# Moving every transpose off the matrix engine: 32x32 squares on VectorE and spreading DMAs in a two-layer encoder trunk

## The chip, the cores and the metric

One core of a Trainium2 chip runs the whole kernel. The metric is device time in microseconds from the start to the end of one execution, as the median of three runs. All arithmetic is float32; matrix products are made in three passes over numbers split into a high part (rounded to the matrix engine's fp32r form) and a low part (the rest).

## The reference, cut to what matters

There are 256 tokens of width 2048, and two layers with pre-norm residuals. The two layers, cut to their core:

```
# even layer
u = rms_norm(h, ln_even_g);  qa, ka, va, qb, kb, vb, gate = split(u @ w_in_even)   # 2048 x 6656
ya = gqa_attention(rope(norm(qa)), rope(norm(ka)), va)                # 8 heads of 128, 2 kv heads
p  = softmax(q1 k1^T*s + bias) - lam * softmax(q2 k2^T*s + bias)      # 8 differential heads, 64 wide
yb = rms_norm(p @ vb, b_subln_g, eps) * (1 - lambda_init)
h  = h + (concat(ya, yb) * silu(gate)) @ w_out_even                   # 2048 x 2048
# odd layer
u = rms_norm(h, ln_odd_g);  qc, kc, vc, gate = split(u @ w_in_odd)    # 2048 x 8192
yc = attention over three dilated windows, 16 heads (a mask and one softmax in the kernel)
h  = h + (yc * silu(gate)) @ w_out_odd;   out = rms_norm(h, final_norm_g)
```

## The kernel before, in words

**Weights.** `job_t` (L163) computes 256 tokens by 512 output columns. Two PSUM banks of the pool `acc` (four banks, so two jobs at a time) take one 128-token tile each. The 2048 rows of the weight come in eight groups. `wgroup` (L135) fetches a group, 128x1024 floats or 512 KB, by one DMA on SyncE's queue into one of four `raw` slots. ScalarE copies it to `hi` (L151), VectorE subtracts to make `lo` (L152), both into one of three slots. Then `mm3` (L157) issues three matmuls of 512 columns for each of 2 k-blocks and 2 token tiles, so twelve for each group. The activations (`u` in layer inputs, `y` in output projections) are the stationary operand.

**Heads.** The projections come out token-major, tokens on partitions. Attention needs q and k with the head width on partitions, and the softmax weights with the keys on partitions. Each such turn is four TensorE transposes of 128x128 against `ident` into one PSUM bank of the pool `att`: `turned` (L228) for a pair of heads' q, k or gate (45 calls), `transposed` (L312) for the weights of one head (32 calls), L388 and L392 for the value rows and norms of the differential heads (`head_b`), and L534 for `tok` at the end of the even layer. ScalarE and VectorE then split the bank into hi and lo (`split`, L208).

`weighted_v` (L328) and `head_b` make the weighted values transposed, width on partitions and 256 tokens in the columns: six matmuls of 256 columns for each head.

**Order.** The instructions are issued in an order that a planner makes from its own costs when the program is built; each engine then keeps that order. Weight splits have raised priority. Heads are spread between the matmuls of the projection that the planner finds ready. SyncE's queue carries weight loads, inputs and the output; SyncE also stands still in order when a load waits for its slot.

In the even layer, for each of two groups: q, gate, four heads of kind A, gate, q, k, value projection, four differential heads. In the odd layer, for each of four groups: gate, q, k, softmax weights of four heads, values, weighted values. After each layer comes the output projection in chunks of columns, each of which goes through all sixteen heads.

Of the kernel before, what the change touches and what calls it, by code (L numbers as in the profile page):

```python
# [10 lines left out]
F32 = mybir.dt.float32  # L11
# [82 lines left out]
def trunk(ctx, tc, x, xt, w_even, w_oe, w_odd, w_oo, gain_cols, rows, final_g, rope_c, geo_c, out):  # L94
# [24 lines left out]
    ones = const.tile([P, P], F32, name="ones")  # L119
    G.memset(ones, 1.0)  # L120
    ident = const.tile([P, P], F32, name="ident")
    make_identity(nc, ident)
# [40 lines left out]
    def job_t(w, c0, wd, a, beside=None, pieces=lambda kg: 1):  # L163

        kn = 1024 // wd
        ps = [acc.tile([P, 512], F32, tag="acc", name=f"acc_t{t}")[:, :wd] for t in range(NT)]
        for kg in range(NK // kn):
# [25 lines left out]
    def square_sum(part, src):  # L193
        sq = work.tile([P, 512], F32, tag="sq", name="sq", bufs=1)[:, :src.shape[-1]]
        A.activation(sq, src, AF.Square, accum_out=part)
# [32 lines left out]
    def turned(z, pair):  # L228

        ps = att.tile([P, 512], F32, tag="att", name="zt")  # L230
        for j in range(2):
            for t in range(NT):
                c = (2 * pair + j) * HD
                T.transpose(ps[:, j * S + t * P:j * S + (t + 1) * P], z[:, t, c:c + HD], ident)  # L234
        return ps.rearrange("p (j k) -> p j k", j=2)

    def pair_t(z, pair, tag, bufs=2):
        ps = turned(z, pair)
        dst = heads.tile([P, 2, 2, S], F32R, tag=tag, name=tag, bufs=bufs)
        split(dst[:, :, 0], dst[:, :, 1], ps)  # L240
        return dst

    def pair_gate(z, pair):
        ps = turned(z, pair)
        gt = heads.tile([P, 2, S], F32, tag="gate", name="gate", bufs=3)
        A.copy(gt, ps)
        return gt
# [3 lines left out]
    def pair_q64(z, pair):  # L251
        ps = turned(z, pair)
        t = heads.tile([P, 2, 2, S], F32R, tag="q", name="q", bufs=2)
        for j in range(2):
            js, other = slice(64 * j, 64 * j + 64), slice(64 - 64 * j, 128 - 64 * j)
            A.activation(t[js, :, j], ps[js], AF.Copy)
            V.tensor_sub(t[other, :, j], ps[js], f(t[js, :, j]))
        return t

    def pair_k64(z, pair):  # L260
        ps = turned(z, pair)
        kh = heads.tile([P, 2, 2, S], F32R, tag="k", name="kh", bufs=2)
        kl = heads.tile([P, 2, 2, S], F32R, tag="k", name="kl", bufs=2)
        for j in range(2):
            js, other = slice(64 * j, 64 * j + 64), slice(64 - 64 * j, 128 - 64 * j)
            A.activation(kh[js, :, j], ps[js], AF.Copy)
            A.activation(kh[other, :, j], ps[js], AF.Copy)
            V.tensor_sub(kl[js, :, j], ps[js], f(kh[js, :, j]))
            A.activation(kl[other, :, j], f(kl[js, :, j]), AF.Copy)
# [19 lines left out]
    def scores(sp, qh, ql, kh, kl):  # L289
        for t in range(NT):  # L290
            ts = slice(t * P, (t + 1) * P)
            o = sp[:, t * S:(t + 1) * S]
            T.matmul(o, qh[:, ts], kh, start=t == 0, stop=False)  # L293
            T.matmul(o, qh[:, ts], kl, start=False, stop=False)  # L294
            T.matmul(o, ql[:, ts], kh, start=False, stop=t == NT - 1)  # L295
# [16 lines left out]
    def transposed(p, ps):  # L312
        for kt in range(NT):
            for t in range(NT):
                T.transpose(ps[:, kt * S + t * P:kt * S + (t + 1) * P], p[:, t, kt * P:(kt + 1) * P], ident)  # L315
        ph = heads.tile([P, NT, S], F32R, tag="ph", name="ph")
        pl = heads.tile([P, NT, S], F32R, tag="pl", name="pl")
        pv = ps.rearrange("p (t k) -> p t k", t=NT)
        split(ph, pl, pv)
        return ph, pl  # L320

    def finish_y(h, src, gate):
        yf = work.tile([P, S], F32, tag="yf", name="yf")
        V.tensor_mul(yf, src, gate)
# [3 lines left out]
    def weighted_v(h, p, v, vs, gate, ps):  # L328
        ph, pl = transposed(p, ps)
        o = ps[:, :S]  # L330
        for kt in range(NT):
            mm3(o, v[:, kt, 0, vs], v[:, kt, 1, vs], ph[:, kt], pl[:, kt], kt == 0, kt == NT - 1)
        finish_y(h, o, gate)

    def head_a(h, q, k, v, vs, gate):
        ps = bank()
        sp = scores(ps, q[:, 0], q[:, 1], k[:, 0], k[:, 1])
# [4 lines left out]
        weighted_v(h, p, v, vs, gate, ps)  # L342
# [32 lines left out]
    def head_b(h, p, v, vs, gate):  # L375
        ps = [bank(), bank()]
        ph, pl = transposed(p, ps[0])
        o = ps[1][:, :S]
        for kt in range(NT):
            mm3(o, v[:, kt, 0, vs], v[:, kt, 1, vs], ph[:, kt], pl[:, kt], kt == 0, kt == NT - 1)  # L380

        on = work.tile([P, S], F32, tag="on", name="on")
        A.copy(on, o)
        ss = small.tile([P, NT], F32, tag="ss", name="ss")
        ot, rb = ps[0][:, :S], ps[0][:, S:]
        for t in range(NT):
            ts = slice(t * P, (t + 1) * P)
            T.transpose(ot[:, ts], on[:, ts], ident)  # L388
            square_sum(ss[:, t:t + 1], ot[:, ts])
        r = rsqrt_mean(ss, HD, SUBLN_EPS, NT, "rb")  # L390
        for t in range(NT):
            T.transpose(rb[:, t * P:(t + 1) * P], r[:, t:t + 1].to_broadcast([P, P]), ident)  # L392
        V.scalar_tensor_tensor(on, on, gsub[:, 0:1], gate, op0=ALU.mult, op1=ALU.mult)
        finish_y(h, rb, on)

    def softmax_c(h, q, k):
        bias = alibi(float(np.exp2(np.float32(-8.0 * (h + 1) / 16))), True)
        sp = scores(bank(), q[:, 0], q[:, 1], k[:, 0], k[:, 1])
        p = biased(sp, bias)
# [68 lines left out]
    def tok_heads(ps, i, n):  # L468
# [3 lines left out]
        for t in range(NT):  # L472
            A.activation(z[:, t], ps[t][:, :n * HD], AF.Copy, scale=rstd[:, t:t + 1])
            sq = work.tile([P, 512], F32, tag="sq", name="sq", bufs=1)[:, :n * HD]
# [22 lines left out]
    for g in range(2):  # L497
        c = 512 * g
        zq = tok_heads(job_t(w_even, c, 512, u) if g else ps_q0, 0, 4)
        zg = gate_t(job_t(w_even, GATE_E + c, 512, u), rh)  # L500
        for pair in range(2):
            q = pair_t(zq, pair, "q")
            gate = pair_gate(zg, pair)
            for j in range(2):
                head_a(4 * g + 2 * pair + j, q[:, j], k_a[:, g], v_a[:, 0], slice(g * HD, g * HD + HD), gate[:, j])
        zg = gate_t(job_t(w_even, GATE_E + 1024 + c, 512, u), rh)
        zq = evac_t(job_t(w_even, B_Q0 + c, 512, u), rs)
        zk = evac_t(job_t(w_even, B_K0 + c, 512, u), rstd)
        v = v_tile()
        ps = []  # L510
        for pair in range(2):
            q = pair_q64(zq, pair)
            kh, kl = pair_k64(zk, pair)
            ps += [softmax_b(4 * g + 2 * pair + j, q[:, j], kh[:, j], kl[:, j]) for j in range(2)]
        evac_v(v, job_t(w_even, B_V0 + c, 512, u), rstd)
        for pair in range(2):
            gate = pair_gate(zg, pair)
            for j in range(2):
                head_b(8 + 4 * g + 2 * pair + j, ps[2 * pair + j], v[:, pair], slice(j * HD, j * HD + HD), gate[:, j])
# [6 lines left out]
    for i, (c0, wd) in enumerate(CHUNKS_E):  # L526
        ps = job_t(w_oe, c0, wd, y_even)
        cs = slice(c0, c0 + wd)
        for t in range(NT):
            V.tensor_add(tok[:, t, cs], tok[:, t, cs], ps[t])  # L530
        for k in range(c0 // P, (c0 + wd) // P):
            ps = att.tile([P, 512], F32, tag="att", name="xps")
            for t in range(NT):
                T.transpose(ps[:, t * P:(t + 1) * P], tok[:, t, k * P:(k + 1) * P], ident)  # L534
            make_u(k, ps[:, :S], gcol[:, NK + k:NK + k + 1])
# [4 lines left out]
    for g in range(4):  # L540
# [4 lines left out]
        zg = gate_t(ps, rh)  # L545
# [94 lines left out]
```

## Time and profile before

| | |
|---|---|
| median of three runs | 920.06 us (919.68 to 920.17) |
| the profiled execution's own time | 919.56 us |
| its span, first to last instruction | 917.8 us |
| TensorE matmul busy | 907.0 us, 99% of the span |
| VectorE busy | 559.6 us, 61% |
| ScalarE busy | 532.6 us, 58% |
| GpSimd busy | 78.2 us, 9% |
| busy share of the 16 DMA engines, SyncE's queue | 50.7% |

1.8 us of the execution's time lie outside the span. Busy times of matmuls overlap, since a matmul's recorded duration includes the pipeline; the distance from one start to the next says what a matmul costs in a row of them.

### The profile page before, as it was taken

The numbers are of one execution on the slowest core, as the hardware profiler recorded it, in microseconds if no ns is written. First come the engines' busy times: TensorE is split into PE (matmuls) and PEld (weight loads), VectorE is DVE, ScalarE is ACT, GpSimd is POOL, SyncE is SP. The second block draws the span as 40 slices with busy tenths as digits, with TensorE's granted clock in tenths as the row PEclk, the third lists the DMA queues.
The fourth block names the chain that finished last, engine by engine and source line by source line (L and its number), as shares of the span: only waits on it lengthen the run. The fifth ranks groups of instructions, "written<-read, shape, count | busy, mean of one in ns | idle before, by whom it ended". The sixth has DMA issues, their size and how long they took to land.

```text
span 917.8 us, 11973 instructions
## 1 busy us (share of the span) xinstructions
PE 907.0 (99%) x4440; PEld 760.4 (83%) x4440; DVE 559.6 (61%) x751; ACT 532.6 (58%) x866; POOL 78.2 (9%) x67
## 2 busy tenths in 40 slices
PE   9999999999999999999999999999999999999996
PEld 7888888888888887888888888888888888888886
DVE  6685644875766686655544765467445754476563
ACT  7657645875576696555544755456544844474451
POOL 0010000110100012000000400032001300040000
PEclk9999999999999999999999999999999999999999
DMA  8855455354544443455555445543554455555552
GB/s 329 311 211 160 154 189 184 138 189 161 179 160 160 171 151 116 169 198 183 184 201 189 154 144 192 196 162 138 186 194 170 147 174 193 193 170 179 194 196 92
DMA packets 47035, 164.39 MB, mean 179 GB/s; under 512 B 5376, under 2 KB 6144, under 8 KB 46976
## 3 DMA queue, kind: packets, MB, share of 16 engines
q1 hardware_dynamic: 46656, 162.57, 50.7%
q0 software_dynamic: 320, 1.05, 0.5%
q8 instruction: 35, 0.57, 0.3%
q14 instruction: 24, 0.20, 0.1%
HBM read 161.50 MB, written 2.10 MB: 178 GB/s over the span
## 4 chain that ended last, share of the span: by engine, by line
PE 96%; ACT 1%; issue 1%; DMA 1%; SPq 0%; DVE 0%; POOLq 0%; POOL 0%; DVEq 0%; ACTq 0%
PE acc_t L160 29%; PE acc_t L161 29%; PE acc_t L159 29%; PE zt L234 2%; PE bank L315 1%; PE bank L159 1%; PE bank L161 1%; PE bank L160 1%; DMA raw<-in_w_in_even 1%; PE bank L294 1%; PE bank L295 1%; PE bank L293 1%; ACT hi L151 0%; PE bank L363 0%; PE bank L364 0%
## 5 line engine op out<-in xcount | busy, mean ns | idle before, releaser
L152 DVE TENSOR_TENSOR lo<-raw,hi 128x1024 fp32r<-128x1024 f32 (+1 forms) x294 | 359.3, 1223 | 284.1 <-ACT hi L151 283.8
L151 ACT ACTIVATE hi<-raw 128x1024 fp32r<-128x1024 f32 (+1 forms) x294 | 309.4, 1054 | 307.7 <-PE acc_t L161 292.0
L160 PE MATMUL acc_t<-lo,u 128*128 128x512 f32 x928 | 364.9, 395 | 0.1
L161 PE MATMUL acc_t<-hi,u 128*128 128x512 f32 x928 | 362.2, 392 | 0.0
L159 PE MATMUL acc_t<-hi,u 128*128 128x512 f32 x928 | 338.4, 393 | 0.4 <-ACT u L183 0.4
L160 PEld LDWEIGHTS acc_t<-lo,u 128*128 128x128 f32 x928 | 174.6, 188 | 36.2 <-DVE lo L152 0.6
L159 PEld LDWEIGHTS acc_t<-hi,u 128*128 128x128 f32 x928 | 174.0, 188 | 36.1 <-ACT u L183 1.2
L161 PEld LDWEIGHTS acc_t<-hi,u 128*128 128x128 f32 x928 | 174.5, 188 | 33.9
L160 PE MATMUL acc_t<-lo,y 128*128 128x512 f32 (+1 forms) x256 | 96.5, 379 | 0.0
L161 PE MATMUL acc_t<-hi,y 128*128 128x512 f32 (+1 forms) x256 | 95.4, 377 | 0.0
L159 PE MATMUL acc_t<-hi,y 128*128 128x512 f32 (+1 forms) x256 | 90.4, 381 | 0.7 <-ACT hi L151 0.6
L351 POOL TENSOR_SCALAR bias<-geo 128x512 f32<-128x512 f32 x24 | 37.5, 1562 | 572.8 <-DVE s L346 534.3
L160 PEld LDWEIGHTS acc_t<-lo,y 128*128 128x128 f32 x256 | 48.3, 189 | 8.6
L159 PEld LDWEIGHTS acc_t<-hi,y 128*128 128x128 f32 x256 | 47.6, 188 | 9.4 <-ACT hi L151 1.4
L161 PEld LDWEIGHTS acc_t<-hi,y 128*128 128x128 f32 x256 | 48.2, 188 | 8.3
L304 ACT ACTIVATE s<-s,nm 128x256 f32<-128x256 f32 x64 | 31.7, 497 | 4.4 <-DVE nm L301 4.3
L216 ACT ACTIVATE z<-acc_t,rstd 128x512 f32<-128x512 f32 x40 | 27.2, 680 | 9.0 <-PE acc_t L161 9.0
L234 PE MATMUL zt<-ident,z 128*128 128x128 f32 x180 | 29.7, 272 | 0.0
L234 PEld LDWEIGHTS zt<-ident,z 128*128 128x128 f32 x180 | 22.4, 140 | 5.0
L346 DVE TENSOR_TENSOR s<-bank,bias 128x512 f32<-128x512 f32 x32 | 21.7, 682 | 6.9 <-POOL bias L353 4.4
L353 POOL TENSOR_TENSOR bias<-bias,geo 128x512 f32<-128x512 f32 x16 | 23.8, 1490 | 1.3
L210 DVE TENSOR_TENSOR pl<-bank,ph 128x512 fp32r<-128x512 f32 x32 | 21.4, 682 | 2.3 <-ACT ph L209 2.2
(137 smaller groups left out, 696.3 us busy)
## 6 DMA issues: line engine op xcount, KB each, us to landing
raw<-in_w_in_odd SPq DMA_DIRECT2D x128, 512.0 KB, 3.2
raw<-in_w_in_even SPq DMA_DIRECT2D x102, 512.0 KB, 3.3
raw<-in_w_out_even SPq DMA_DIRECT2D x32, 512.0 KB, 3.2
raw<-in_w_out_odd SPq DMA_DIRECT2D x32, 512.0 KB, 3.2
tok<-in_x SPq DMA_DIRECT2D x4, 512.0 KB, 8.8
xk<-in_xt SPq DMA_DIRECT2D x6, 256.0 KB, 6.7
raw<-in_w_in_even SPq DMA_DIRECT2D x4, 256.0 KB, 4.0
gf<-in_final_norm_g POOLq DMA_DIRECT2D x4, 256.0 KB, 4.7
```

The costliest lines, as they stand in the source:

```text
L151: A.activation(hi[:, ks], rv[:, ks], AF.Copy)
L152: splits.append(V.tensor_sub(lo[:, ks], rv[:, ks], f(hi[:, ks])))
L159: T.matmul(ps, ah, bh, start=start, stop=False)
L160: T.matmul(ps, ah, bl, start=False, stop=False)
L161: T.matmul(ps, al, bh, start=False, stop=stop)
L210: V.tensor_sub(lo, src, f(hi))
L216: A.activation(z[:, t], ps[t], AF.Copy, scale=r[:, t:t + 1])
L234: T.transpose(ps[:, j * S + t * P:j * S + (t + 1) * P], z[:, t, c:c + HD], ident)
L304: A.activation(e[:, t], s[:, t], AF.Exp, bias=nm[:, t:t + 1], accum_out=den[:, t:t + 1])
L346: V.tensor_add(s, sp, bias)
L351: G.tensor_scalar_mul(b, geo[:, 0], -slope)
L353: G.tensor_add(b, b, geo[:, 1])
```

## The change

All 372 TensorE transposes go. The new `turned` takes a 128 x 2 x 256 token-major tile. Two VectorE transposes, of 256 elements on each partition, turn every 32x32 square of it into a scratch tile `x` (two slots). Four DMAs on SyncE's queue, one for each 32 source partitions, then spread it over all 128 partitions of `pt` (three slots) or `gate`; each moves 64 KB in 128 pieces of 512 bytes. The readers that split into hi and lo now read this tile in SBUF, in an order of quarters.

The differential heads make their weighted values token-major, with the turned weights stationary and 128 value columns moving (twelve matmuls for each head), so their norm needs no turning; the finished product of a pair of heads is turned once. Queries and gates are turned sooner, while a later projection runs. The output projections start with two column chunks for the first twelve heads and then do the last four heads for both (`jobs_out`). To make room, `raw` has three slots in place of four.

```diff
-        raw = wpool.tile([P, 1024], F32, tag="raw", name="raw", bufs=4)
+        raw = wpool.tile([P, 1024], F32, tag="raw", name="raw", bufs=3)
...
+    def jobs_out(w, chunks, a):
+
+        (c0, wd), (c1, _) = chunks[:2]
+        ps = [job_banks(wd) for _ in range(2)]
+        for kgs in (range(6), range(6, 8)):
+            for p, c in zip(ps, (c0, c1)):
+                job_steps(p, w, c, wd, a, kgs)
+        for i, (c, wd) in enumerate(chunks):
+            yield i, slice(c, c + wd), ps[i] if i < 2 else job_t(w, c, wd, a)
...
-    def turned(z, pair):
-
-        ps = att.tile([P, 512], F32, tag="att", name="zt")
-        for j in range(2):
-            for t in range(NT):
-                c = (2 * pair + j) * HD
-                T.transpose(ps[:, j * S + t * P:j * S + (t + 1) * P], z[:, t, c:c + HD], ident)
-        return ps.rearrange("p (j k) -> p j k", j=2)
+    def turned(src, tag="pt", bufs=3):
+
+        x = work.tile([P, 4, 4, 32], F32, tag="x", name="x", bufs=2)
+        for m in range(2):
+            V.transpose(x[:, :, 2 * m:2 * m + 2].rearrange("p b t c -> p t b c"),
+                        src[:, :, m * P:(m + 1) * P].rearrange("p t (r b) -> p t b r", b=4))
+        dst = heads.tile([P, 4, 4, 32], F32, tag=tag, name=tag, bufs=bufs)
+        for a in range(4):
+            nc.sync.dma_start(dst[:, a].rearrange("p n c -> p (n c)"), x[32 * a:32 * a + 32].rearrange("r b n c -> r (b n c)"))
+        return dst.rearrange("p a n c -> p n a c")
...
-    def pair_gate(z, pair):
-        ps = turned(z, pair)
-        gt = heads.tile([P, 2, S], F32, tag="gate", name="gate", bufs=3)
-        A.copy(gt, ps)
-        return gt
...
+    def pair_b(h, ps, v, zg):
+
+        os = []
+        ss = small.tile([P, 8], F32, tag="ss8", name="ss4", bufs=2)[:, :2 * NT]
+        for j in range(2):
+            ph, pl = weights_t(ps[j])
+            vs = slice(j * HD, j * HD + HD)
+            o = bank()[:, :S].rearrange("p (t e) -> p t e", t=NT)
+            for t in range(NT):
+                ts = slice(t * P, (t + 1) * P)
+                for kt in range(NT):
+                    mm3(o[:, t], ph[:, kt, ts], pl[:, kt, ts], v[:, kt, 0, vs], v[:, kt, 1, vs], t == kt == 0, t == kt == 1)
+            for t in range(NT):
+                square_sum(ss[:, 2 * j + t:2 * j + t + 1], o[:, t])
+            os.append(o)
+        r = rsqrt_mean(ss, HD, SUBLN_EPS, 2 * NT, "rb")
+        yt = stile()
...
+        yt = turned(yt)
+        for j in range(2):
+            y[h + j] = acts.tile([P, 2, S], F32R, tag="y", name="y")
+            times_turned(y[h + j][:, 0], y[h + j][:, 1], yt[:, 2 * j:2 * j + 2], gsub[:, 0:1])
...
-    for i, (c0, wd) in enumerate(CHUNKS_E):
-        ps = job_t(w_oe, c0, wd, y_even)
-        cs = slice(c0, c0 + wd)
+    for i, cs, ps in jobs_out(w_oe, CHUNKS_E, y_even):
...
-        for k in range(c0 // P, (c0 + wd) // P):
-            ps = att.tile([P, 512], F32, tag="att", name="xps")
-            for t in range(NT):
-                T.transpose(ps[:, t * P:(t + 1) * P], tok[:, t, k * P:(k + 1) * P], ident)
-            make_u(k, ps[:, :S], gcol[:, NK + k:NK + k + 1])
+        for k in range(cs.start // P, cs.stop // P, 2):
+            xk = turned(tok[:, :, k * P:k * P + S])
...
```

## Rows read from the trace of the kernel before

**Rows 1.** The page: busy time of each engine, and the chain that ended last.
```profile
PE 907.0 (99%) x4440; PEld 760.4 (83%) x4440; DVE 559.6 (61%) x751; ACT 532.6 (58%) x866; POOL 78.2 (9%) x67
...
PE 96%; ACT 1%; issue 1%; DMA 1%; SPq 0%; DVE 0%; POOLq 0%; POOL 0%; DVEq 0%; ACTq 0%
```

**Rows 2.** Waits, longest first: engine, line, waited for: us in total, times, longest.
```profile
ACT hi L151 <- PE acc_t L161: 292.0, 216, 2.8
...
PE acc_t L159 <- ACT hi L151: 0.6, 1, 0.6
```

**Rows 3.** Timeline of PE: start us, duration us, instruction; three stretches.
```profile
0.98 4.63 PE L130 MATMUL idle<-ones 128*128 128x128 f32 x20 [0.98 <-POOL ones L120]
5.27 1.20 PE L159 MATMUL acc_t<-hi,u 128*128 128x512 f32 x2
...
189.65 0.39 PE L161 MATMUL acc_t<-hi,u 128*128 128x512 f32 x1
...
189.88 0.60 PE L315 MATMUL bank<-ident,s 128*128 128x128 f32 x4
...
190.55 0.40 PE L160 MATMUL acc_t<-lo,u 128*128 128x512 f32 x1
...
902.80 0.28 PE L159 MATMUL acc_l<-u,y 128*128 128x256 f32 x1
902.92 0.28 PE L160 MATMUL acc_l<-u,y 128*128 128x256 f32 x1
```

**Rows 4.** The chain that ended last in order of time: start us, us, what.
```profile
115.61 0.45 PE acc_t L159 x2
118.33 0.45 PE acc_t L159 x2
```

**Rows 5.** Groups on PE, shapes apart: count, busy us, mean ns, idle before.
```profile
L160 PE MATMUL acc_t<-lo,u 128*128 128x512 f32 x928 | 364.9, 395 | 0.1
...
L234 PE MATMUL zt<-ident,z 128*128 128x128 f32 x180 | 29.7, 272 | 0.0
L315 PE MATMUL bank<-ident,s 128*128 128x128 f32 x128 | 20.7, 272 | 0.0
L160 PE MATMUL bank<-pl,v 128*128 128x256 f32 x48 | 13.7, 286 | 0.0
...
L388 PE MATMUL bank<-ident,on 128*128 128x128 f32 x16 | 4.4, 280 | 0.3 <-ACT on L383 0.3
...
L534 PE MATMUL xps<-ident,tok 128*128 128x128 f32 x32 | 4.4, 274 | 0.1
...
L392 PE MATMUL bank<-ident,rb 128*128 128x128 f32 x16 | 2.9, 272 | 0.0
```

**Rows 6.** Groups on DVE, shapes apart.
```profile
L152 DVE TENSOR_TENSOR lo<-raw,hi 128x1024 fp32r<-128x1024 f32 x290 | 356.6, 1231 | 282.3 <-ACT hi L151 282.0
L301 DVE TENSOR_REDUCE nm<-s 128x2 f32<-128x512 f32 x32 | 21.8, 680 | 0.4
...
L486 DVE TENSOR_TENSOR t<-z,rq 128x256 f32<-128x256 f32 x8 | 3.0, 417 | 0.0
...
L605 DVE TENSOR_SCALAR tok<-tok,r 128x256 f32<-128x256 f32 x2 | 0.7, 354 | 0.9 <-POOL r L598 0.9
```

**Rows 7.** Windows of 20 us: length, busy us (count) of PE, PEld, DVE, ACT, POOL; PEclk, DMA, GB/s.
```profile
160.00:180.00 20.00, 20.00 (x101) 16.79 (x100) 16.49 (x27) 16.29 (x34) 2.99 (x2) 1.00 0.38 132
180.00:200.00 20.00, 20.00 (x106) 16.99 (x105) 17.93 (x30) 16.50 (x36) 3.82 (x2) 1.00 0.54 190
...
320.00:340.00 20.00, 20.00 (x103) 16.81 (x102) 18.20 (x31) 19.28 (x41) 2.99 (x2) 1.00 0.37 129
340.00:360.00 20.00, 18.77 (x99) 15.00 (x98) 14.91 (x31) 14.24 (x38) 6.53 (x5) 1.00 0.46 160
```

**Rows 8.** Groups on ACT, shapes apart.
```profile
L151 ACT ACTIVATE hi<-raw 128x1024 fp32r<-128x1024 f32 x290 | 306.9, 1059 | 304.8 <-PE acc_t L161 292.0 <-issue 5.8 <-DMA raw<-in_w_in_even 4.7
...
L246 ACT COPY gate<-zt 128x512 f32<-128x512 f32 x16 | 9.3, 581 | 1.4 <-PE zt L234 1.2
```

**Rows 9.** Timeline of SyncE's queue (SPq) at the start.
```profile
2.12 0.43 SPq L149 DMA_DIRECT2D raw<-in_w_in_even  x1
2.59 0.43 SPq L422 DMA_DIRECT2D xk<-in_xt  x1
```

**Rows 10.** The page: SyncE's DMA queue, and issues (count, KB each, us to landing).
```profile
q1 hardware_dynamic: 46656, 162.57, 50.7%
...
raw<-in_w_in_odd SPq DMA_DIRECT2D x128, 512.0 KB, 3.2
...
out<-tok SPq DMA_DIRECT2D x2, 128.0 KB, 1.9
```

**Rows 11.** DMA in the window 906 to 917.8 us, output stores alone.
```profile
DMA packets 1152, 2.10 MB, mean 178 GB/s; under 512 B 128, under 2 KB 384, under 8 KB 1152
...
q1 hardware_dynamic: 1152, 2.10, 48.4%
```

More of the change, by code (lines that the diff above doesn't have):

```diff
@@ L8 @@
 from concourse import mybir
-from concourse.masks import make_identity
 F32 = mybir.dt.float32
@@ L193, in square_sum @@
     def square_sum(part, src):
-        sq = work.tile([P, 512], F32, tag="sq", name="sq", bufs=1)[:, :src.shape[-1]]
+        sq = work.tile([P, 512], F32, tag="th", name="sq", bufs=1)[:, :src.shape[-1]]
         A.activation(sq, src, AF.Square, accum_out=part)
@@ L310, in stile, with weights_t, weighted_v, softmax_a @@
         return work.tile([P, 512], F32, tag="s", name="s", bufs=4).rearrange("p (t k) -> p t k", t=NT)
-    def transposed(p, ps):
-        for kt in range(NT):
-            for t in range(NT):
-                T.transpose(ps[:, kt * S + t * P:kt * S + (t + 1) * P], p[:, t, kt * P:(kt + 1) * P], ident)
+    def weights_t(p):
+        ps = turned(p)
         ph = heads.tile([P, NT, S], F32R, tag="ph", name="ph")
         pl = heads.tile([P, NT, S], F32R, tag="pl", name="pl")
-        pv = ps.rearrange("p (t k) -> p t k", t=NT)
-        split(ph, pl, pv)
+        split(quarters(ph), quarters(pl), ps)
         return ph, pl
-    def finish_y(h, src, gate):
+    def weighted_v(h, p, v, vs, gate):
+        ph, pl = weights_t(p)
+        o = bank()[:, :S]
+        for kt in range(NT):
+            mm3(o, v[:, kt, 0, vs], v[:, kt, 1, vs], ph[:, kt], pl[:, kt], kt == 0, kt == NT - 1)
         yf = work.tile([P, S], F32, tag="yf", name="yf")
-        V.tensor_mul(yf, src, gate)
+        V.tensor_mul(row_quarters(yf), row_quarters(o), gate)
         y[h] = acts.tile([P, 2, S], F32R, tag="y", name="y")
         split(y[h][:, 0], y[h][:, 1], yf)
[L328 to L337, printed above, removed]
+    def softmax_a(q, k):
+        sp = scores(q, k)
         p = stile()
@@ L341, in head_a @@
             A.activation(p[:, t], p[:, t], AF.Copy, scale=rden[:, t:t + 1])
[L342 removed]
+        return p
     def biased(sp, bias):
@@ L373, in softmax_b @@
         return p
[L375 to L394, printed above, removed]
+    def pair_b(h, ps, v, zg):
[7 more added lines that the diff above has]
+                ts = slice(t * P, (t + 1) * P)
+                for kt in range(NT):
+                    mm3(o[:, t], ph[:, kt, ts], pl[:, kt, ts], v[:, kt, 0, vs], v[:, kt, 1, vs], t == kt == 0, t == kt == 1)
+            for t in range(NT):
+                square_sum(ss[:, 2 * j + t:2 * j + t + 1], o[:, t])
[3 more added lines that the diff above has]
+        for j in range(2):
+            c = slice(j * HD, j * HD + HD)
+            for t in range(NT):
+                V.scalar_tensor_tensor(yt[:, t, c], os[j][:, t], r[:, 2 * j + t:2 * j + t + 1], zg[:, t, c], op0=ALU.mult,
+                                       op1=ALU.mult)
+        yt = turned(yt)
+        for j in range(2):
+            y[h + j] = acts.tile([P, 2, S], F32R, tag="y", name="y")
+            times_turned(y[h + j][:, 0], y[h + j][:, 1], yt[:, 2 * j:2 * j + 2], gsub[:, 0:1])
@@ L545, in trunk @@
         zg = gate_t(ps, rh)
+        gates = [turned(cols(zg, pair), "gate") for pair in range(2)]
         zq = evac_t(job_t(w_odd, c, 512, u), rs)
+        qs = [pair_t(zq, pair, "q") for pair in range(2)]
         zk = evac_t(job_t(w_odd, D + c, 512, u), rstd)
@@ L549, in trunk @@
         for pair in range(2):
-            q = pair_t(zq, pair, "q")
             k = pair_t(zk, pair, "k")
-            p += [softmax_c(4 * g + 2 * pair + j, q[:, j], k[:, j]) for j in range(2)]
+            p += [softmax_c(4 * g + 2 * pair + j, qs[pair][:, :, j], k[:, :, j]) for j in range(2)]
         v = v_tile()
```

87 lines of the change are left out of this document (50 added, 37 removed).

## The prediction

> **What bounds the kernel now.** Three views, in this order. First the page's busy times and the chain that ended last: matmuls are busy 99% of the span and make 96% of the chain, and no engine but TensorE is over 61% [rows 1]. A busy matmul engine can still be waiting, so next the waits: ScalarE stands still 292 us for TensorE to give `hi` slots back, while a matmul waits for `hi` once, 0.6 us [rows 2]. Everything else is early and TensorE is late. Third, since matmul durations overlap, the starts in the timeline give the price of each kind [rows 3]. A 256-column matmul costs 0.12 us (902.80 to 902.92). From 189.65 to 190.55 lie two matmuls of 512 columns and four transposes. A group of twelve 512-column matmuls repeats every 2.72 us where nothing lies between [rows 4], so 0.227 us each; that leaves 0.90 - 0.45 = 0.45 us for four transposes, 0.11 us each. So TensorE is a full queue, and what leaves it is worth its pace, not its recorded 272 ns.
>
> **What the change removes.** Transposes by line: 180 + 128 + 16 + 32 + 16 = 372 [rows 5]. At 0.11 us: 372 x 0.11 = 40.9 us off TensorE. They lie in its queue between matmuls and none is hidden by anything, so all of it is on the path.
>
> The rule that speaks against this: the Trainium skill, "VectorE: DVE Perf Modes", sections "The three transpose paths" and "Rules for kernel authors", says that a 128x128 transpose belongs on TensorE where PSUM is a fit place for it, since VectorE turns only 32x32 blocks. It gives 390 ns on TensorE and 311 ns on VectorE in bf16 for that size. By 390 ns the removal would be worth an estimated 145 us, by the rows' pace 41 us; the rows are this kernel's own, with transposes in a full queue, so they decide. By 311 ns the 340 squares would cost VectorE an estimated 106 us, which lies inside the bounds below.
>
> **What it adds on TensorE.** The eight differential heads made their weighted values with six matmuls of 256 columns each, in the groups of `bank` from `v` as in [rows 5]: 48 x 0.12 = 5.8 us. They now take 12 each, 96 of 128 columns. No row has that shape in fp32r. Bounds: half of the 256-column price, 0.06 us (5.8 us, no change); and the plain fp32 warm-up products of 128 columns, whose 20 records fill 0.98 to 5.27 us, 0.21 us each [rows 3] (20.6 us). I take 0.11, the price of the transposes, which are 128 columns and load a 128x128 stationary operand each: 10.6 us. So +4.8 us, between 0 and +14.8.
>
> **What it adds on VectorE.** `turned` is called 85 times: 37 in the even layer (one for k of kind A, then 18 in each of two groups), 8 for the new `u`, 40 in the odd layer. That is 170 transposes of 256 elements per partition. No row shows one. Nearest below: a one-input operation of 128x256, 0.354 us; nearest in kind, a strided SBUF operation of 128x256, 0.417 us; above, as if each element were handled twice, a 128x512 pass, 0.680 us [rows 6]. I take 0.417: 71 us, between 60 and 116. VectorE then has 560 + 71 = 631 us (620 to 676) of about 885, some 71%. Off TensorE's path on average, because it waits 282 us for ScalarE today [rows 6]. But not everywhere: in the stretch of the differential softmax it is busy 34.4 of 40 us in the first group and 33.1 of 40 in the second [rows 7]. There six of the turns fall (two k, four weights), 12 x 0.417 = 5.0 us, which makes 39.4 and 38.1 of 40. ScalarE is at 19.28 of 20 in the same place, and in the second group TensorE already loses 1.2 us behind it. I put 2.5 us of new TensorE waits on each of the two stretches: +5 us. The low end is 0 (the turns of q and weights move into neighbouring stretches), the high end 5 us each, as if VectorE stood still for all of it.
>
> **ScalarE** loses the 16 gate copies, 9.3 us [rows 8], and gains nothing of that size: off the path, worth 0 while it waits for TensorE as in [rows 2]. The other vector work of the differential heads is about even (four 128-column products and four low parts for a pair, in place of three 256-column ones for each head).
>
> **What it adds on SyncE's queue and the DMA engines.** 85 x 4 = 340 DMAs. Issued back to back, one takes 0.47 us from start to start [rows 9]: 160 us beside today's 290 full weight loads, counted by their subtractions [rows 6], at 136 us; together a third of the span, so not the bound. A turn keeps SyncE for 1.9 us. Data: 340 x 64 KB = 22.3 MB in 43,520 packets. By bytes that adds 22.3/162.6 of 50.7%, 7% [rows 10]; by packets, the stores at the end give 0.484 x 11.8 x 16 / 1152 = 79 ns for a mean packet of 1.8 KB [rows 11], so at most 215 us of the 16 engines, 23%. Either way under 75% in all. Price 0.
>
> Where the new waits stand: SyncE stops at a turn's first DMA until VectorE has transposed, and the weight loads queue behind it; VectorE stops at a transpose until an `x` slot is read out, and the `lo` subtractions queue behind it; ScalarE stops at a split until the data has landed, and the `hi` copies queue behind it. Three `raw` slots are 8.2 us of TensorE's work ahead, and a load lands in 3.2 us [rows 10]: 5 us of slack for SyncE, of which a turn's issue uses 1.9. With four slots it was 7.7. ScalarE and VectorE are up to two further slots (5.4 us) ahead of TensorE, less the 2.3 us of one pair of passes [rows 6, 8]. I charge nothing for these. At the very start a load that used to be fetched into the fourth slot comes later; 0 to 1.3 us, inside the range.
>
> **Latency of a turn.** Before, 0.45 us on TensorE. After: 2 x 0.417 + 4 x 0.47 + about 1.9 us to land, as the 128 KB store [rows 10] = 4.6 us, so 4.1 us more for each hop. The next projection covers it: 21.8 us of matmuls that need none of these heads. For the last heads of a layer the new order gives 12 of 16 groups (six for each of two chunks), 32.7 us in place of 16.3. Price 0 for as long as the planner's order has other matmuls in front.
>
> **Sum.** 919.6 (the profiled execution's own time, 0.5 under the median) - 40.9 + 4.8 + 5 = 888.5; I say 888. With all low ends 919.6 - 40.9 = 879; with all high ends 919.6 - 40.9 + 14.8 + 10 + 1.3 = 905.
>
> **The rivals.**
>
> *The hops show.* The planner puts a head's matmul where it believes the data to be ready; if the landing takes longer than it believes, TensorE stands at that place in its order. There are about 20 such hops in series: k of kind A, q/k and weights of two A groups (4), k, weights and y of two differential groups (6), `u`, k and weights of four odd groups (8). One microsecond too little at each is 20 us: 888 + 20 = 908. For it: heads stand in TensorE's order close to when they become ready, and a turn issued behind a weight load shares its 3.2 us landing. Against it: in the odd layer weights are turned beside the value projection, which must end first anyway.
>
> *VectorE's turns cost more than they free.* The hop as a whole is exposed: 4.1 us at each of 20 places, 883.5 + 82 = 965. It decides against the change from 36.1 / 20 = 1.8 us of exposed wait at each hop. For it: VectorE at 90% in the differential stretch [rows 7] and three engines in order with a wait on each. Against it: 282 us in which VectorE waits, 292 in which ScalarE does. The rule of the Trainium skill, "VectorE: DVE Perf Modes", section "Rules for kernel authors", that a full 128x128 transpose goes to TensorE would hold here in this way; so far the trace bears out only that TensorE's price is small.
>
> *No stalls, and 128 columns at half the price of 256.* 879 us.
>
> *The change moves nothing* would need the transposes to have cost TensorE no time; their starts exclude that. Landing within 0.2% of before (about what a measurement of this kernel can tell from no change) would be chance.
>
> **How the numbers follow.** The forecast with its own range of 880 to 897: 0.58. No stalls, below 880: 0.07. Hops partly exposed, 897 to 918: 0.20. Within 0.2%: 0.03. Hops exposed in full, slower: 0.12. So faster 0.85, same 0.03, slower 0.12. The range 879 to 911 takes the forecast, most of the no-stall case near its edge and most of the partly exposed one: about 0.8.
>
> **What would show it.** Right: no 128x128 f32 transposes on TensorE; its start-to-start time in weight groups still 2.72 us; few waits on TensorE, at the differential stretches; VectorE near 630 us; transposes at about 0.42 us each. The 128-column products at 0.11 us from start to start. Wrong: TensorE rows with waits for `ph`, `q` or `k` of microseconds, repeated for each group (hops); ScalarE waiting for `pt` with `hi` copies behind it; SyncE's queue waiting for a transpose with `raw` loads late; a VectorE transpose over 0.68 us.

## The result, and the profile after

The changed kernel takes 929.73 us (median of four runs, 929.34 to 930.33), the kernel before, beside it, 919.87: a ratio of 1.0109, 95% interval 1.0091 to 1.0126. The change makes the kernel about 1% slower, where 888 was forecast. The profiled execution took 929.34 us with a span of 927.6.

The page of after, busy times, slices, queues, the chain and DMA issues, against [rows 1, 10]:

```profile
PE 885.8 (95%) x4116; PEld 734.8 (79%) x4116; DVE 647.9 (70%) x941; ACT 522.5 (56%) x842; POOL 91.2 (10%) x61
...
PE   9998999999999988498999999999999999999996
...
PEclk9999999999999999698999999999999999999999
...
q1 hardware_dynamic: 95616, 184.87, 61.2%
...
PE 50%; DVE 16%; DMA 12%; ACT 7%; SPq 7%; issue 6%; POOL 1%; DVEq 0%; ACTq 0%; POOLq 0%
...
raw<-in_w_in_odd SPq DMA_DIRECT2D x128, 512.0 KB, 4.2
...
pt<-x SPq DMA_DIRECT2D x292, 64.0 KB, 2.2
```

TensorE makes 50% of the chain that ended last, where it made 96%. A kernel that was one full queue has become a kernel that waits: slice 17 (371 to 394 us) shows TensorE at 4 tenths and the clock at 6.

How much it waits is worked out from TensorE's timeline: each distance from one start to the next, less the price of the matmuls between (0.227, 0.12 and 0.11 us for 512, 256 and 128 columns), summed over the kernel up to the last matmul. This "lost time" (the sums are good to some 3 us) is 7.8 us before, over half of it at the start and 2.3 us between 340 and 360, and 53.7 us after. In 43 of the 46 stretches of 20 us of before, with none to 24 transposes in them, and in 29 of after, it is within 0.3 us of nothing, so the prices hold. The rest of the span is then counts times prices, and that it falls by 53.7 - 7.8 - (927.6 - 917.8) = 36.1 us, the forecast's -40.9 + 4.8, follows from the working and is no second measurement. For the same reason the sum over a kernel says little more than its span; what it adds is where the time goes. The miss is lost time: 45.9 us more of it, where 5 were charged. 28.2 us of it lie between 360 and 440 us, 6.5 at 320, 4.6 at 80, 4.2 between 240 and 280.

The waits of after, of PE, of ACT, and of SyncE's queue (us in total, times, longest), against [rows 2]:

```profile
PE acc_t L156 <- ACT y L261: 14.0, 2, 9.1
PE acc_t L156 <- ACT hi L148: 10.1, 3, 6.6
PE acc_t L157 <- DVE lo L149: 4.4, 8, 1.0
PE bank L388 <- ACT kh L296: 2.0, 3, 0.9
...
ACT hi L148 <- DMA raw<-in_w_in_odd: 60.9, 43, 6.5
ACT hi L148 <- DMA raw<-in_w_in_even: 38.3, 30, 4.7
...
SPq L251 <- DVE x L247: 43.6, 38, 3.3
SPq L146 <- DMA raw<-in_w_in_odd: 27.5, 17, 2.4
```

Two things are new. ScalarE waits 99 us for the weight loads of the two layers' inputs, where [rows 8] have 4.7 for the even layer's; TensorE then waits for `hi`. And TensorE waits 14.0 us, twice, for `y`, the last heads of the even layer.

**Where a load comes late.** Timeline of after, first SyncE's queue and ScalarE, then TensorE, around 88 us:

```profile
75.12 0.33 SPq L146 DMA_DIRECT2D raw<-in_w_in_even  x1
76.19 6.38 SPq L251 DMA_DIRECT2D pt<-x  x8
82.67 2.48 SPq L251 DMA_DIRECT2D gate<-x  x4
85.25 1.50 SPq L146 DMA_DIRECT2D raw<-in_w_in_even  x3
...
89.50 1.06 ACT L148 ACTIVATE hi<-raw 128x1024 fp32r<-128x1024 f32 x1 [4.65 <-DMA raw<-in_w_in_even]
...
88.13 0.39 PE L158 MATMUL acc_t<-hi,u 128*128 128x512 f32 x1
90.61 0.73 PE L156 MATMUL acc_t<-hi,u 128*128 128x512 f32 x2 [2.09 <-ACT hi L148]
...
404.86 12.29 SPq L251 DMA_DIRECT2D pt<-x  x16
```

Turns come in runs. A "spread" is one of a turn's four DMAs. Twelve of them stand here in a row, four in 2.48 us, 0.62 us each, and eight in 6.38, 0.80 each with waits for VectorE between; sixteen at 404.86 (the new `u`) take 12.29 us. Between two loads lie 10.1 us here and 13.4 there (403.80 to 417.20); the longest run, twenty spreads from 311.95, keeps two loads 14.4 us apart, ahead of the 6.5 us lost at 320. Three `raw` slots are 8.2 us of TensorE's work, and a load lands after 4.2 us, not 3.2. So `hi` is late, and TensorE with it.

**Where `y` comes late.** The chain that ended last, in order of time:

```profile
373.54 0.79 PE acc_t L156
...
377.75 0.42 PE acc_t L156
378.17 0.23 PE acc_t L157
...
383.90 0.13 PE bank L158
384.11 0.38 ACT sq L208 x2
384.51 0.38 ACT sq L208 x2
384.91 0.18 DVE rb L202
385.16 1.02 POOL rb L203
386.20 1.13 DVE s L420 x4
387.33 1.05 DVE x L247 x2
388.40 0.56 SPq L251
...
389.66 0.59 SPq L251
390.30 2.15 DMA pt<-x
392.55 0.52 ACT y L261
393.11 0.79 PE acc_t L156
393.90 0.43 PE acc_t L157
```

VectorE before it (timeline):

```profile
359.15 0.87 DVE L397 SCALAR_TENSOR_TENSOR s<-s,rden 128x256 f32<-128x256 f32 x2
...
366.63 2.17 DVE L247 STREAM_TRANSPOSE x<-s 128x256 f32<-128x256 f32 x4
...
373.00 1.16 DVE L247 STREAM_TRANSPOSE x<-s 128x256 f32<-128x256 f32 x2 [1.96 <-DMA pt<-x]
```

From the last product of the second pair (383.90) to the first matmul that takes its `y` (393.11) lie 9.2 us with nothing on TensorE: sums of squares, norm, scaling, and the turn, 5.1 us from 387.33. The first pair had the same wait before 373.54 (4.95 us). They come in series: the second pair's weights are ready at 355.2 and 360.0, but VectorE turns them only behind the first pair's product, one in the run of four transposes from 366.63 (two for the product, two for the weights) and the other at 373.00, so that pair's products start at 381.23. By then the twelve groups of the first twelve heads (144 matmuls from 322.6 to 368.4) and those of the first pair (24, from 373.54) are used up. The restart is slow too: ten matmuls from 373.54 to 378.17 take 4.63 us, 0.43 each behind the first; at the usual pace (0.39 for the first, 0.227 for each other) that would be 2.4, so 2.2 us more go. The granted clock says why; windows of after, columns as in [rows 7]:

```profile
92.00:94.00 2.00, 2.00 (x5) 1.61 (x6) 1.55 (x2) 2.00 (x4) 0.00 (x0) 0.50 0.58 172
...
388.00:392.00 4.00, 0.00 (x0) 0.00 (x0) 0.38 (x1) 0.00 (x0) 0.00 (x0) 0.50 0.36 94
392.00:396.00 4.00, 2.89 (x7) 2.31 (x8) 1.14 (x4) 0.91 (x2) 0.00 (x0) 0.50 0.00 1
```

It is 0.50, the 1.2 GHz level, during or behind a stall, where [rows 7] have 1.00 throughout. Matmuls in after that wait for nothing and still start further apart than their price, under a granted clock of 0.50, make some 12 us of the 53.7.

**VectorE's turns.** Groups on DVE, shapes apart, against [rows 6]:

```profile
L247 DVE STREAM_TRANSPOSE x<-z 128x256 f32<-128x256 f32 x82 | 45.5, 605 | 0.6 <-DVE lo L149 0.3
L247 DVE STREAM_TRANSPOSE x<-s 128x256 f32<-128x256 f32 x72 | 41.6, 617 | 4.5 <-DMA pt<-x 3.6 <-ACT s L366 0.8
```

### The profile page after: what moved, and what is told of

Read it like the earlier page. It is cut to its first block, busy times and chain, and to the rows that moved or that the text cites. A ratio compares the mean times of both kernels' runs of the same rounds, so it can differ in the third digit from the quotient of the medians.

```text
span 927.6 us, 12116 instructions
## 1 busy us (share of the span) xinstructions
PE 885.8 (95%) x4116; PEld 734.8 (79%) x4116; DVE 647.9 (70%) x941; ACT 522.5 (56%) x842; POOL 91.2 (10%) x61
## 3 DMA queue, kind: packets, MB, share of 16 engines
q1 hardware_dynamic: 95616, 184.87, 61.2%
## 4 chain that ended last, share of the span: by engine, by line
PE 50%; DVE 16%; DMA 12%; ACT 7%; SPq 7%; issue 6%; POOL 1%; DVEq 0%; ACTq 0%; POOLq 0%
PE acc_t L157 16%; PE acc_t L158 15%; PE acc_t L156 15%; DVE lo L149 6%; SPq L251 6%; ACT hi L148 4%; DMA pt<-x 4%; DVE x L247 4%; DMA raw<-in_w_in_odd 4%; DMA raw<-in_w_in_even 2%; DMA tok<-in_x 1%; DVE nm L332 1%; DVE s L371 1%; ACT s L335 1%; DMA raw<-in_w_out_odd 1%
## 5 line engine op out<-in xcount | busy, mean ns | idle before, releaser
L158 PE MATMUL acc_t<-hi,u 128*128 128x512 f32 x928 | 361.5, 391 | 0.0
L156 PE MATMUL acc_t<-hi,u 128*128 128x512 f32 x928 | 330.6, 392 | 4.6 <-ACT hi L148 3.6
L156 PE MATMUL acc_t<-hi,y 128*128 128x512 f32 (+1 forms) x256 | 93.0, 393 | 20.8 <-ACT y L261 14.0
L376 POOL TENSOR_SCALAR bias<-geo 128x512 f32<-128x512 f32 x24 | 48.7, 2029 | 551.6 <-DVE s L371 508.1
L157 PE MATMUL acc_t<-lo,y 128*128 128x512 f32 (+1 forms) x256 | 100.4, 392 | 1.1 <-DVE lo L149 1.0
L158 PE MATMUL acc_t<-hi,y 128*128 128x512 f32 (+1 forms) x256 | 97.3, 384 | 0.0
L156 PEld LDWEIGHTS acc_t<-hi,y 128*128 128x128 f32 x256 | 50.0, 197 | 31.5 <-ACT y L261 14.6
L158 PEld LDWEIGHTS acc_t<-hi,y 128*128 128x128 f32 x256 | 49.4, 193 | 8.8
L247 DVE STREAM_TRANSPOSE x<-z 128x256 f32<-128x256 f32 x82 | 45.5, 605 | 0.6 <-DVE lo L149 0.3
L247 DVE STREAM_TRANSPOSE x<-s 128x256 f32<-128x256 f32 x72 | 41.6, 617 | 4.5 <-DMA pt<-x 3.6
L222 ACT ACTIVATE ph<-pt 128x512 fp32r<-128x512 f32 x32 | 20.2, 631 | 35.4 <-DMA pt<-x 34.9
L223 DVE TENSOR_TENSOR pl<-pt,ph 128x512 fp32r<-128x512 f32 x32 | 23.3, 729 | 12.3 <-ACT ph L222 12.2
L378 POOL TENSOR_TENSOR bias<-bias,geo 128x512 f32<-128x512 f32 x16 | 27.7, 1731 | 1.3
```

The lines of the kernel that those rows point to most:

```text
L156: T.matmul(ps, ah, bh, start=start, stop=False)
L157: T.matmul(ps, ah, bl, start=False, stop=False)
L158: T.matmul(ps, al, bh, start=False, stop=stop)
L223: V.tensor_sub(lo, src, f(hi))
L247: V.transpose(x[:, :, 2 * m:2 * m + 2].rearrange("p b t c -> p t b c"), src[:, :, m * P:(m + 1) * P].rearrange("p t (r b) -> p t b r", b=4))
L376: G.tensor_scalar_mul(b, geo[:, 0], -slope)
```

## The experiments

Theory: the loss is two waits, late loads behind runs of spreads, and the two turns in series at the end of the even layer. Rivals: the hops of all heads are exposed; VectorE's turns; the third `raw` slot by itself; the products' extra PSUM banks. Every edit also lets the planner make a new order for the whole kernel, so a wait can vanish in one place and another appear elsewhere; lost time and waits are read for that reason beside the time. Lost time is that of the profiled execution, which in the kernels that spread most lies some us from the median (b_values_first: 909.51 us, median 914.03).

| run | edit | median us | ratio to before, 95% | lost time us |
|---|---|---|---|---|
| after | the change | 929.73 | 1.0091 to 1.0126 | 53.7 |
| b_values_first | products of both pairs, then both turns | 914.03 | 0.9904 to 0.9952 | 34.8 |
| a_one_bank | kind A: one PSUM bank for each head | 931.77 | 1.0122 to 1.0152 | 56.3 |
| act_queue | spreads on ScalarE's queue | 948.21 | 1.0278 to 1.0317 | 74.4 |
| before_raw3 | before, three `raw` slots | 920.88 | 1.0002 to 1.0021 | 8.6 |
| odd_turns | before, turns in the odd layer alone | 913.74 | 0.9919 to 0.9952 | 20.4 |
| values_u | values first, `u` turned on TensorE | 915.10 | 0.9937 to 0.9967 | not summed |
| values_act | values first, spreads on ScalarE | 930.95 | 1.0107 to 1.0146 | 58.8 |
| values_split | values first, spreads on two queues | 900.24 | 0.9770 to 0.9815 | 21.8 |
| split_only | spreads on two queues | 917.47 | 0.9962 to 0.9986 | 42.2 |
| values_split_bank | values_split and one bank | 904.52 | 0.9817 to 0.9878 | 28.6 |
| values_split_plain | values_split, old order of the output projection | 905.11 | 0.9795 to 0.9852 | 28.8 |
| values_split_y | values_split, `y` turned on TensorE | 903.63 | 0.9785 to 0.9872 | 24.7 |
| pt2_raw3 | two `pt` slots | 929.57 | 1.0088 to 1.0122 | 53.8 |
| pt2_raw4 | two `pt` slots, four `raw` | 906.36 | 0.9838 to 0.9867 | 30.7 |
| raw4_values | pt2_raw4, values first | 892.97 | 0.9691 to 0.9723 | 17.4 |
| raw4_split | pt2_raw4, two queues | 922.42 | 1.0018 to 1.0040 | 51.3 |
| raw4_values_split | all three | 898.67 | 0.9761 to 0.9790 | 23.0 |

**1. The order of the two pairs.** `pair_b` is cut in two, so that the second pair's weights are turned before the first pair's product.

```diff
-            pair_b(8 + 4 * g + 2 * pair, ps[2 * pair:2 * pair + 2], v[:, pair], cols(zg, pair))
+        pv = [pair_values(ps[2 * pair:2 * pair + 2], v[:, pair]) for pair in range(2)]
+        for pair in range(2):
+            pair_y(8 + 4 * g + 2 * pair, *pv[pair], cols(zg, pair))
```

> Edit: the changed kernel, but in each group of differential heads the weighted values of both pairs are written before the norm, turn and split of either pair's product, so that scratch and PSUM slots are given to the weight turns of the second pair first. Theory 1 (slots are handed out in program order, so the second pair's weights could not be turned before the first pair's product had been): the two waits for y at the end of the even layer, 5.0 and 9.1 us with some 5 us of half clock behind them, go; 929.7 - 19 = 911 us. Rival (each turn is simply slow, VectorE and the landing set the chain): the first wait stays and the second shrinks by half at most; 924 us or more.

15.7 us less than after, and 0.7% faster than before. No wait for `y` stands in the list any more; waits for `hi` stay (7.7 us, the longest 3.8):

```profile
PE acc_t L156 <- ACT hi L148: 7.7, 7, 3.8
PE acc_t L157 <- DVE lo L149: 5.2, 10, 0.7
```

The serial turns are shown as a cause, and shown not to be the whole.

**2. One PSUM bank for a head of kind A.**

```diff
-                p = softmax_a(qs[pair][:, :, j], k_a[:, :, g])
+                ps = bank()
+                p = softmax_a(qs[pair][:, :, j], k_a[:, :, g], ps)
```

(the product is then written to `ps` too)

> Edit: the changed kernel, but each head of kind A writes its weighted values into the PSUM bank of its scores again, as before the change. Theory 1: the four heads no longer come 15 us apart in TensorE's order (82.6, 104.2, 119.3, 134.3 us in the changed kernel), their scores start together, the differential heads of the second group start some 10 us sooner, and the first wait for y (5.0 us and 2.4 us of clock) goes, the second stays: 922 us. Rival (SyncE's queue alone): nothing moves, 929 us; the waits at 88 and 258 us stay in both.

A miss: `y` costs 3.8 us in place of 14.0, but 12.0 us of waits for `hi`, 8.2 for `lo` and 3.8 for `ph` stand there instead. The time does not fall (its interval overlaps that of after): closing kind A's spacing moves the waits and does not remove them.

**3. Spreads on another queue.** ScalarE's, in full (act_queue; with values first, values_act), or by halves (split_only, values_split).

```diff
-            nc.sync.dma_start(dst[:, a]...
+            (nc.sync if a < 2 else nc.scalar).dma_start(dst[:, a]...
```

> Edit: the changed kernel with the 340 spreading DMAs issued from ScalarE's queue in place of SyncE's. Theory 2 (a weight load stands behind 12 to 16 spreading DMAs of 0.64 us each in SyncE's queue, longer than three slots last): the waits of TensorE for hi at 88, 258, 415 us and the small ones at 670 and 845 go, 21 us in all with the clock behind them; 909 us. Rival: ScalarE, 56% busy, now stops at each DMA until VectorE has transposed, and its hi copies come late; no gain or slower, 930 to 950 us. The waits for y at the end of the even layer stay.

> Edit: as b_values_first, with the spreading DMAs issued from ScalarE's queue. In act_queue the weight loads were on time (TensorE waited 2.6 us for hi in place of 10.1) but heads came later in the order and waits for y and ph took 34 us. Theory 1: with values first the 19 us for y go, the 15 for ph partly stay: 948 - 25 = 923 us, not better than 914. Theory 2 alone (SyncE's queue is all that is left): 900 us.

> Edit: the changed kernel, with two of each turn's four spreading DMAs issued from SyncE's queue and two from ScalarE's, and the order of the heads' steps as in the change. Both theories together: the waits for hi behind bursts in SyncE's queue go (the waits at 88, 258 and 415 us with their half clock, 4.6 + 4.2 + 8.9 us, and some 4 us in the odd layer), the waits for y at the end of the even layer stay (19 us): 929.7 - 20 = 910 us, 10 us over values_split. If SyncE's queue were the only cause, 900 us, as values_split.

> Edit: as b_values_first, with two of each turn's four spreading DMAs issued from SyncE's queue and two from ScalarE's. Theory 2: SyncE is kept half as long by a burst of turns, the weight loads behind it come on time, the waits for hi go (7.7 us and clock): 904 us. Rival (ScalarE stops at the DMAs, hi comes late instead): 914 us or more.

With every spread on ScalarE's queue, loads are on time (waits for `hi` 2.6 and 3.1 us), but turns are late: TensorE waits 15.1 and 11.6 us for `ph`, and the time rises, to 931 in values_act, where 923 was expected. ScalarE is in order, so a spread there stands until VectorE has transposed, and `hi` copies wait with it (14.5 us for `x` in act_queue). By halves the time falls, 12.3 us alone (7 us short of what was expected) and 13.8 us with values first (4 us more); the waits of values_split:

```profile
PE bank L156 <- ACT ph L222: 4.2, 3, 2.9
PE acc_t L156 <- ACT y L261: 3.5, 1, 3.5
```

No wait for `hi` is left there. The Trainium skill, "DMA: Bandwidth & Descriptors", section "Issuing engines are not separate DMA queues", says that a second issuing engine saves only the time to initiate a DMA, usually small beside the DMA itself. The first half agrees: spreads on two queues land no sooner (2.8 and 3.0 us in values_split, 2.2 in after). The second does not hold here, where that time is not small, 0.62 us a spread beside 2.2 us to land, 340 times.

**4. The kernel before, changed a little.** `raw` with three slots; and with that the odd layer alone on the new turns (q, k, gate and weights there, as in the change; smaller scratch tiles shared to make room).

```diff
-        raw = wpool.tile([P, 1024], F32, tag="raw", name="raw", bufs=4)
+        raw = wpool.tile([P, 1024], F32, tag="raw", name="raw", bufs=3)
...
-            q = pair_t(zq, pair, "q")
-            k = pair_t(zk, pair, "k")
+            k = pair_s(zk, pair, "k")
```

> Edit: the kernel before with three raw slots in place of four, nothing else. Theories 1 and 2: without spreading DMAs in SyncE's queue three slots are enough, within 1 us of before, 920 to 921 us. Rival (the lost slot alone makes weight loads late): 5 us or more slower.

> Edit: the kernel before, with three raw slots, its even layer and its output projections as before (TensorE transposes), and only the odd layer's q, k, gate and weight turns made by VectorE and spreading DMAs (40 turns, 160 transposes fewer). Theory 1 (the turn pays where a later projection covers its latency; the loss is the even layer's chain): 920.9 (three slots alone) - 160 x 0.111 = 17.8, + 4.5 us of odd-layer waits as in the changed kernel's trace after 440 us: 908 us. Rival (turns cost as much as they free everywhere): 916 us or more.

The third slot alone costs 1.1 us: without spreads three slots are enough. The odd layer's turns alone gain 6.1 us, where 908 was expected: 6.8 us are lost again at 820 and 2.2 at 740, with 4.3 us of waits for `hi`. So hops between the odd layer's heads are not exposed as such, and late loads appear there too.

**5. Smaller variations on values first.** `u` turned on TensorE; one bank; the output projection in plain order; `y` turned on TensorE.

```diff
-            xk = turned(tok[:, :, k * P:k * P + S])
+            xk = turned_pe(tok[:, :, k * P:k * P + S])
...
-        for kgs in (range(6), range(6, 8)):
-            for p, c in zip(ps, (c0, c1)):
-                job_steps(p, w, c, wd, a, kgs)
+        for p, c in zip(ps, (c0, c1)):
+            job_steps(p, w, c, wd, a, range(8))
...
-        yt = turned(yt)
+        yt = turned_pe(yt)
```

> Edit: as b_values_first, and the 8 turns of the new u at the end of the even layer go back to TensorE (32 transposes, 3.5 us). Theory 2 (the wait at 394 us, 5.8 us with its clock, 2.0 in the next slice, is a weight load behind the 16 spreading DMAs of u): 914 - 7.8 + 3.5 = 910 us, and no wait for hi of over 1 us after 380 us. Rival (that wait is for u itself or for the bandwidth): the wait stays, 917 us.

> Edit: as values_split, and the heads of kind A write weighted values into the bank of their scores again. In a_one_bank the four heads' turns came in one burst and SyncE's queue made them late (14 us of waits between 100 and 120 and between 280 and 300 us), which ate what the earlier differential heads gave. Theory: with the burst on two queues half of that remains and the wait for kh at 311 us (3.0 us) and part of those at 357 to 365 us (8.9 us) go; 896 us. Rival: bursts still late on two queues, 902 us or more.

> Edit: as values_split, but each output projection takes its first column chunk through all sixteen heads before the second (the order before the change). The prediction counted the new order as 16.4 us more cover for the last heads. If it is needed, TensorE waits some 12 to 16 us more at the end of the even layer and a few at the end of the odd one: 915 us. If the chain of the heads is short enough without it, 900 us.

> Edit: as values_split, but the finished product of a pair of differential heads is turned by 4 TensorE transposes in place of VectorE and four DMAs (16 transposes more, 1.8 us). If the turn's latency is what TensorE waits for at the end of the even layer (357 to 365 us, 8.9 us with clock, 3.5 of it for y), half goes: 897 us. If the wait is for the weights of the second pair, 902 us.

None gains. With `u` on TensorE the wait at 380 to 400 goes (-0.2 us there), as the theory of sixteen spreads in a row has it, but 9.7 us at 160 and 7.5 at 300 come in the new order, with 5.6 us of waits for `kh`: the total missed its 910. With the plain order of the output projection the time is 4.9 us higher, where 15 were expected if the new order was needed; turning `y` on TensorE leaves `y` waits at 1.8 us and still ends 3.4 us higher. Both intervals overlap that of values_split, so neither difference is clear of noise. One bank ends 4.3 us higher, where 4 less were expected.

**6. The fourth `raw` slot.** Two `pt` slots in place of three make the room; pt2_raw3 is the control.

```diff
-    def turned(src, tag="pt", bufs=3):
+    def turned(src, tag="pt", bufs=2):
...
-        raw = wpool.tile([P, 1024], F32, tag="raw", name="raw", bufs=3)
+        raw = wpool.tile([P, 1024], F32, tag="raw", name="raw", bufs=4)
```

> Edit: the changed kernel with two pt slots in place of three; the control for pt2_raw4. The heads come somewhat later in the order, so the waits for y grow: 930 to 940 us. The waits for hi behind SyncE's bursts stay as in the changed kernel (88, 258, 415 us).

> Edit: as pt2_raw3 with four raw slots, as before the change. If the lost slot is part of the cause (a burst of twelve spreading DMAs keeps SyncE from a weight load for 10.1 us; three slots last 8.2 us, four 10.9 us), the waits at 88 and 258 us go with their half clock (4.6 + 4.2 us) and the one after sixteen DMAs shrinks by 2.7 us: 10 us under pt2_raw3. If bursts are not what makes the loads late, the same as pt2_raw3.

929.57 - 906.36 = 23.2 us for one slot of 512 KB, more than twice what was expected, and 20 times its worth without spreads (1.1 us, experiment 4). SyncE's queue has the same burst (8 and 4 spreads from 73.73 to 82.51) and the loads land no sooner (4.3 us), but TensorE waits for none of them, and ScalarE's waits for the layers' input loads are 19 us, 99 in after; what is left is `y`. Waits of pt2_raw4:

```profile
PE acc_t L156 <- ACT y L261: 19.3, 2, 10.2
PE bank L158 <- DVE pl L223: 2.0, 1, 2.0
...
ACT hi L148 <- DMA raw<-in_w_in_even: 11.1, 8, 3.8
...
ACT hi L148 <- DMA raw<-in_w_in_odd: 8.2, 5, 2.5
```

Outside of the start (4.4 us) and 340 to 400 us (26.4), next to no lost time remains, in both layers and for all the other heads.

**7. Both cures together.**

> After the change with two turn slots, a fourth raw slot, and the weighted values of both pairs of differential heads ahead of both turns. Theory (two causes explain the whole loss: weight loads late behind the spreads, which the fourth slot cures, and the end of the even layer, which the order of the pairs cures): the fourth slot alone left 906.4, of which 19.3 us are waits for y at the end of the even layer with the half clock behind them, so 906 - 19 = 887, between 884 and 892; no TensorE wait for y over 2 us and none for hi. Rival (the waits for y only move to another product, as they did with the value rows turned on TensorE): 900 to 908, with new waits for ph, kh or lo of several microseconds.

> Two turn slots, a fourth raw slot, and the spreads shared between SyncE's and ScalarE's queues. Theory: with four slots no load is late any more, so the second queue has nothing left to give: 906, between 902 and 910, and the waits for y of some 19 us stay. Rival (the second queue helps by landing a turn earlier, not by freeing the loads): the waits for y shrink to under 10 us and the time to 896 or less.

> All three edits. Theory: as the fourth slot with both pairs' values first, 887, between 883 and 892, the queue being worth under 3 us beside the slot. Rival (slot and queue cure different waits, and add up): 5 us or more under the version without the second queue.

892.97 us, 2.9% under before (0.9707), the fastest kernel of the study. The waits for `y` fall to 4.0 us and none for `hi` stands. It is 1 us above the expected range: 13.0 us of lost time remain between 340 and 380. Waits and windows of raw4_values:

```profile
PE acc_t L156 <- ACT y L261: 4.0, 2, 2.3
PE bank L156 <- ACT ph L222: 1.1, 1, 1.1
```

```profile
340.00:360.00 20.00, 16.89 (x82) 13.99 (x82) 17.25 (x32) 11.96 (x34) 4.34 (x3) 0.87 0.69 203
360.00:380.00 20.00, 16.92 (x56) 13.02 (x57) 9.29 (x22) 5.81 (x9) 1.01 (x1) 0.79 0.29 90
```

The waits there are short (the longest 2.3 us), but the granted clock falls behind them (0.87 and 0.79 on average), which makes some 5.6 of the 13.0 us. The two queues beside the fourth slot are a loss: 5.7 us with values first, 16.1 without, where both theories had none or a gain. Loads were on time in both; in raw4_split `y` costs 17.3 and 3.0 us and `ph` 5.2. So slot and second queue cure the same wait and do not add. Why the second queue then costs, by ScalarE standing at spreads or only by the planner's other order, these runs do not separate.

## Why the prediction was wrong

**Right: what the transposes and the 128-column products cost.** -40.9 and +4.8 gave -36.1. The prices behind it hold: with them next to nothing is left in most stretches of either kernel. The products start every 0.11 us in the timeline of after (381.40, 381.51, 381.62, 381.73).

**Off, without harm: VectorE.** A transpose takes 0.61 us, not 0.417, 96.3 us in all with the 16 of `tok` (9.2 us, 614 ns each), inside the bounds of 60 to 116; VectorE's 648 us lie inside 620 to 676. The Trainium skill, "VectorE: DVE Perf Modes", section "The three transpose paths", gives 311 ns for 128x128 in blocks of 32x32 on VectorE in bf16, so two would be an estimated 0.62 us. The trace agrees (605 to 617 ns, in f32). The 390 ns that the same table has for TensorE is not what a transpose costs in a full queue, 0.11 us. The rival "VectorE's turns cost more than they free" had the right sign by the wrong mechanism: it put 4.1 us at each of 20 places, while TensorE waits long for a turn at two, both times for `y`.

**Near: the differential stretches.** Charged 5 us, 2.5 for each. In after the second loses 6.5 us (320 to 340; waits for `kh` and `lo`, and the half clock behind them), the first next to nothing (0.6 between 180 and 200). With the fourth slot nothing is lost at 320, so full engines alone, the reason given, are not shown to be its cause.

**Wrong: "5 us of slack for SyncE, of which a turn's issue uses 1.9", charged at nothing.** The step took one turn at a time, 0.47 us a DMA and a landing of 3.2 us. Turns come three to five in a row, at 0.62 to 0.80 us a DMA, so a load can stand 10.1 to 14.4 us behind the load before it, against 8.2 us of slots, and lands after 4.2. Measured by the fourth slot: 23.2 us, the clock behind the stalls included. The prediction named late `raw` loads among the signs of being wrong, and gave no rival for them. The removal of a slot was put at 0 to 1.3 us, at the start; that is its price without spreads (1.1), not with them.

**Wrong: "Price 0 for as long as the planner's order has other matmuls in front".** The latency was near (5.1 us against 4.6), and for nearly all heads the cover held: pt2_raw4 loses next to nothing outside of 340 to 400 us. At the end of the even layer it did not. The 32.7 us of cover were there (the 144 matmuls) and were set against one hop, but two chains of turns stand in series (weights, norm, `y`, and again), because the second pair's weights are turned behind the first pair's product. Values first, with the loads already on time, gives back 13.4 us.

**Not charged at all: the half clock.** Every stall of two microseconds or more in after, and some shorter ones, are paid again in part: 2.2 us behind 373.54, some 12 us in all. These 12 us are inside the shares below, not beside them.

Sum, by lost time in this order of the edits (two `pt` slots change it by 0.1): of 45.9 us, 23.1 are late loads (53.8 to 30.7), 13.3 the order of the pairs (30.7 to 17.4), and 9.6 stay, at 340 to 380 (13.0 there, 2.6 before). In the other order values first comes out at 18.9 and the slot at 17.4 (53.7, 34.8, 17.4): the two losses overlap, and only their sum of 36.3 does not hang on the order. With both mended the kernel takes 893 us, inside the forecast's own range of 880 to 897: what the change takes off TensorE was right, the two covers charged at nothing were not. What the last 9.6 us need stays open.

## What to carry to other kernels

A queue's slack is to be compared with the longest run of new work in front of a load, not with one piece of it: twelve cheap DMA issues outlast three slots. Do not pay for a change that puts work in a prefetch queue with a slot of that prefetch; here one slot turned a loss of 1% into a gain of 1.5%. Where the last heads before a layer's end feed each other through shared buffers, write all that is ready ahead of what waits, so that latencies run side by side.

## What the runs showed of the hardware

A spread of 64 KB inside SBUF holds SyncE's queue 0.62 us when they follow each other without a wait, against 0.47 us for the issues in [rows 9], and lands after 2.2 us (after). With 340 of them the 512 KB loads of the odd layer land after 4.2 us in place of 3.2, though the queue's packets take but 61.2% of the DMA engines' time; what makes them land later was not tried by itself. A VectorE transpose of 256 f32 elements on each of 128 partitions takes 605 to 617 ns. TensorE's granted clock was 0.50 of full speed in or behind stalls as short as 1.5 us (258.71 to 260.58 in after), with matmuls of 512 columns every 0.43 us for the next 2 to 5 us; behind one of 1.4 us in pt2_raw3 (up to 90.67) it stayed at 1.00.
